# A hybrid decoder layer on one core: block inverse per pair of heads, earlier chains, another order of head groups

## The chip, the core and the metric

The kernel runs on one core of a Trainium2 chip. The core has TensorE (PE, with its weight loads as PEld), VectorE (DVE), ScalarE (ACT), GpSimd (POOL) and SyncE (SP); each runs its own instructions in order and waits for the others by semaphores. The metric is the device time of one execution in microseconds (us), as a median of several runs. A profile of one execution stands beside it.

## What is computed

A decoder layer on 16 meta tokens and 256 tokens of width 2048, in float32. Eight pairs of heads go through RWKV-7 time mixing, eight through stick-breaking attention; then come an output projection, LayerNorm, a gated MLP with a convolution, and LayerNorm. The part that matters here is the recurrence of the time mixing:

```python
def step(S, inp):
    r_t, dec_t, k_t, v_t, kk_t, a_t = inp
    sa = jnp.einsum('bhvk,bhk->bhv', S, -kk_t)
    S = (S * dec_t[:, :, None, :] + sa[..., None] * (kk_t * a_t)[:, :, None, :]
         + v_t[..., None] * k_t[:, :, None, :])
    return S, jnp.einsum('bhvk,bhk->bhv', S, r_t)
...
p = h @ w_in[l]
y_rwkv = rwkv7_mixer(p[..., :RWKV_COLS], ...)
y_sb = stick_breaking_mixer(p[..., RWKV_COLS:], sb_norm_g[l])
mix = jnp.concatenate([y_rwkv, y_sb], axis=-1) @ w_out[l]
h = layer_norm(DEEPNORM_ALPHA * h + mix, ln1_g[l], ln1_b[l])
```

## The kernel before

The layer runs in one pass. Weights come by SP's DMA queue in pieces of 512 KB; ACT and DVE split each into a high and a low part (`whi`, line 183, and `wlo`, line 186), and PE makes three products per tile of them (lines 479 to 483 inside the woven part, 227 to 229 outside of it). The stages are: embedding LayerNorm and the small projections (to about 62 us), the woven part (to about 564 us), the rest of the output projection with LayerNorm, the up projection, and the down projection (to the end).

**The woven part.** `ORDER` lists 16 groups: R0 to R7, each a pair of heads of the time mixing, and S0 to S7, each a pair of the stick-breaking attention ("sticks"). Each group has three projections, each of 48 matmuls on PE. Between them the small work is woven in: `weave` counts matmuls, and after every 16 of them a slot comes (`SLOT`), in which tasks that are due may put their next part into PE's order. A task says with `yield` after how many slots it wants to go on. So the order of PE is fixed when the program is built (`manual_schedule` holds it), while the other engines' orders are set by a scheduler. PE can't pass over an instruction that waits.

**One pair of the time mixing.** The 288 padded tokens are 9 blocks of 32 (`NCH`, `CH`). `rwkv_front` makes the decays and the normalised keys (its product `ss` is a head-wise sum on PE). `rwkv_back` makes the `gram` products of each block on PE (line 621) and masks them on DVE (AG, line 623). The upper half of a block's gram is a strictly triangular 32 x 32 matrix, and the chain needs the inverse of one minus it. POOL computes that inverse: two DMAs write the masked blocks to DRAM (`dl`, line 628), others load them as `LT` (line 631) with one block on each partition, and `inverse` then runs 31 steps of two instructions (lines 670 and 672): multiply a column of `Y` with a row of `LT` into `ytmp`, add it to `Y`. `Y` begins as the identity, loaded from a constant (line 601). The result goes to DRAM (`dy`, line 673) and from there to `TT` (line 678).

Before, this is done for two pairs of heads at once: two pairs are 36 blocks (`NB`), and each block stands on three partitions (`RG`) of which each holds 11 of the 32 rows (`NR`): row n on group n modulo 3. That is 108 partitions. `blocks` gives the two pairs one `LT` and one `Y`, and `inverse` runs when the second pair's blocks are loaded.

**The chains.** `chain(q)` walks the 9 blocks for pairs 2q and 2q+1: on PE a product with AG (line 697), one with the inverse TT (line 706), one that moves the state on (line 718), with copies on ACT and DVE between. It begins when `rwkv_back` of the odd pair has ended, and its first yield is `INVERSE` = 18 slots, so that the inverse has time. TT has two buffers, one for even and one for odd q. LT, Y and ytmp have one each.

Other names: `wide` hands out large tiles from two pools and chooses the pool by how many are in use; `mix` tiles are what the output projection reads; `MEAN` says after which of the steps of the first up projection (three matmuls each) the sums of x and of x squared (p1 and p2, line 1038) are taken on PE; POOL adds up what they read (lines 973 and 974).

Of the kernel before, what the change touches and what calls it, by code (L numbers as in the profile page):

```python
# [9 lines left out]
F32 = mybir.dt.float32  # L10
F32R = mybir.dt.float32r
AF = mybir.ActivationFunctionType
ALU = mybir.AluOpType
PSUM = bass.MemoryType.PSUM

P = 128
# [9 lines left out]
CH = 32  # L26
NCH = TP // CH
# [5 lines left out]
NEG = -1.0e30  # L33
EARLY = 8
SLOT = 16
INVERSE = 18
UNITS = 16
MEAN = 8
LATER = 8
AHEAD = 300  # L40
WARM = 42
# [4 lines left out]
GN_EPS, SB_EPS = 64e-5, 1e-6  # L46
ALPHA = 2.0 ** 0.25
DECAY = float(np.exp(-0.5))
NB = 36
RG = 3  # L50
NR = 11

ORDER = [(x[0], int(x[1])) for x in "R0 R1 R2 R3 S0 S1 R4 R5 S2 R6 R7 S3 S4 S5 S6 S7".split()]

KTS = [0, 1, 2, 3, 4, 5, 8, 9, 10, 11, 12, 13, 6, 7, 14, 15]
SBW = NQ + 144 + 16
# [8 lines left out]
for _name, _w in _PV:  # L65
# [4 lines left out]
_CV = [("ident", 128), ("maskg", 2 * CH), ("sbmask", SBW), ("reset", TP),  # L70
       ("tri", 128), ("bd", 128), ("cen", 128), ("ones", 128), ("y0", NR * CH)]
CV = {}
# [7 lines left out]
def constants():  # L80
    c = np.zeros((P, NCV), np.float32)

    def put(name, a):
        o, w = CV[name]
        c[: a.shape[0], o:o + w] = a

    i = np.arange(P)
    put("ident", np.eye(P))
    put("bd", (i[:, None] // 64 == i[None] // 64) / 32)
    put("ones", np.ones((P, P)))  # L90
    put("tri", i[:, None] >= i[None])
    s, t, kind = i[:, None] % CH, i[None, :2 * CH] % CH, i[None, :2 * CH] // CH
    put("maskg", np.where(kind == 0, s < t, s <= t))
    put("cen", np.eye(P) - (i[:, None] // 64 == i[None] // 64) / 64)
    m = np.full((P, SBW), NEG, np.float32)
    for n, (k0, c0, c1, q0) in enumerate(ZB):
        key, q = k0 + i[:, None], q0 + np.arange(c1 - c0)[None]
        ok = key < q
        if n == 2:
            ok &= key >= 256  # L100
        m[:, c0:c1][ok] = 0
    put("sbmask", m)
    r = np.ones((P, TP))
    r[:, ::CH] = 0
    put("reset", r)
    y0 = np.zeros((RG, NB, NR, CH))
    for n in range(CH):
        y0[n % RG, :, n // RG, n] = 1
    put("y0", y0.reshape(RG * NB, NR * CH))
    return c  # L110

# [2 lines left out]
def hybrid_layer(ctx, tc, xin, cst, pvec, w2a2, g2, ln2, w_in, w_out, w_up, w_down, out, dbg=None):  # L114
    nc = tc.nc
    V, S, G, PE = nc.vector, nc.scalar, nc.gpsimd, nc.tensor
    mm = PE.matmul

    def pool(stack, name, **kw):
        return stack.enter_context(tc.tile_pool(name=name, bufs=1, reuse_waits="tile", **kw))  # L120
# [117 lines left out]
    def mtile(dtype, name):  # L238
        return hp.tile([P, 2, TP], dtype, tag="m", bufs=2 * NPAIR, name=name)
# [6 lines left out]
    ncc, nce = CV["y0"][0], CV["tri"][0]  # L246
# [37 lines left out]
    with ExitStack() as es:  # L284
# [88 lines left out]
        o = PV["mu_r"][0]  # L373
# [64 lines left out]
    dp = pool(astack, "dp", space=bass.MemoryType.DRAM)  # L438
# [3 lines left out]
    FULL, SQUARE, HALF_COLS, QUARTER_COLS = range(4)  # L442
# [51 lines left out]
    used = [NPAIR, 0]  # L494
# [5 lines left out]
    def persistent(name, shape):  # L500
        t = ap2.tile(shape, F32, name=name)
        G.memset(t, 0.0)
        return t


    TT = [persistent(f"TT{p}", [P, NCH, 2 * CH]) for p in range(2)]
# [3 lines left out]
    def atile(name, shape, bufs=1):  # L510
        return ap2.tile(shape, F32, tag=name, bufs=bufs, name=name)
# [11 lines left out]
    urow = [slice(64, 96), slice(0, 32)]  # L523
# [25 lines left out]
    def wide(name, dtype=F32, n=None):  # L549

        if n is None:
            n = int(used[1] < UNITS)
        place_of[name] = n
        used[n] += 1
        assert used[n] <= (2 * NPAIR, UNITS)[n], (name, place_of)
        return mtile(dtype, name) if n == 0 else ap2.tile([P, 2, TP], dtype, tag="m", bufs=UNITS, name=name)

    def rwkv_front(j, st):

        a = sg[j][:, 1]  # L560
        sq = atile("sq", [P, TP])
        S.activation(sq, k_, AF.Square, scale=par("k_k", j))
        sq = halves(sq, "rn", "ss")
        cum = atile("cum", [P, TP])
        V.tensor_tensor_scan(out=cum, data0=reset, data1=sg[j][:, 0], initial=0.0, op0=ALU.mult, op1=ALU.add)
        S.activation(Pt[:, :, 1:], ch(cum), AF.Exp, scale=-DECAY)
        Pinv = cum
        S.activation(Pinv, cum, AF.Exp, scale=DECAY)
        yield 2, FULL, 1
        ps = misc("ss")  # L570
        by_head(ps[:, :TP], *sq)
        ss = atile("ss", [P, TP])
        V.tensor_scalar(out=ss, in0=ps[:, :TP], scalar1=16.0, scalar2=0.5e-24, op0=ALU.mult, op1=ALU.max)
        rn = atile("rn", [P, TP])
        S.activation(rn, ss, AF.Ln, scale=2.0 * KSC)
        S.activation(rn, rn, AF.Exp, scale=-0.5, bias=lnb[:, 1:2])
        y2 = atile("sq", [P, TP])
        S.activation(y2, rn, AF.Square)
        V.tensor_mul(ss, ss, y2)
        V.scalar_tensor_tensor(rn, ss, 1.5, rn, op0=ALU.subtract, op1=ALU.mult)  # L580
        kkn = rn
        V.scalar_tensor_tensor(kkn, k_, par("k_k", j), rn, op0=ALU.mult, op1=ALU.mult)
        ba = atile("ss", [P, TP])
        V.scalar_tensor_tensor(ba, kkn, -1.0, a, op0=ALU.mult, op1=ALU.mult)
        kp = st["kp"] = atile("kp", [P, TP])
        S.activation(kp, a, AF.Identity, scale=par("k_a", j), bias=omka[:, j:j + 1])
        give(f"sg{j}")
        V.tensor_mul(kp, kp, k_)
        BK = st["BK"] = wide(f"BK{j}", n=0).rearrange("p n t -> p (n t)").rearrange("p (c x t) -> p c x t", x=2, t=CH)
        V.tensor_mul(BK[:, :, 0], ch(ba), ch(Pinv))  # L590
        V.tensor_mul(BK[:, :, 1], ch(kp), ch(Pinv))
        st["kkn"] = kkn

    solved, bonus = {}, {}
    dl = dp.tile([4, NCH, CH, CH], F32, name="dl")
    dy = dp.tile([NB, NR * RG, CH], F32, name="dy")

    def blocks(q):
        if q not in solved:
            solved[q] = atile("LT", [P, CH, CH]), atile("Y", [P, NR, CH])  # L600
            nc.gpsimd.dma_start(solved[q][1][:RG * NB].rearrange("p r t -> p (r t)"), cst[:RG * NB, ncc:])
        return solved[q]

    def rwkv_back(j, st):

        BK = st["BK"].rearrange("p c x t -> p c (x t)")
        AG = st["AG"] = [wide(f"AG{j}{x}").rearrange("p n t -> p (n t)").rearrange("p (c t) -> p c t", c=NCH) for x in range(2)]
# [15 lines left out]
                V.tensor_mul(AG[x][t, c0:c0 + n], ps[t, :n], maskg[t].unsqueeze(1).to_broadcast([64, n, 2 * CH]))  # L623

        V.tensor_mul(BK, BK, PC.unsqueeze(2).to_broadcast([P, NCH, 2 * CH]))
        LT, Y = blocks(j // 2)
        for x in range(2):
            nc.gpsimd.dma_start(dl[j % 2 * 2 + x].rearrange("c s t -> s c t"), AG[x][urow[x], :, :CH])
        for g in range(RG):
            o = g * NB + j % 2 * 2 * NCH  # L630
            nc.gpsimd.dma_start(LT[o:o + 2 * NCH], dl[j % 2 * 2:j % 2 * 2 + 2].rearrange("x c s t -> (x c) s t"))
        if j % 2:
            inverse(j // 2, LT, Y)
        yield 1, FULL, 1
        ps = misc("bonus")
        by_head(ps[:, :NQ], *rk)
# [23 lines left out]
        for h, t in zip(heads, toks):  # L660
            V.tensor_copy(BT[t, NCH - 1], pv_[:64, 3, h])

    def inverse(q, LT, Y):

        tmp = atile("ytmp", [P, NR, CH])
        n_ = RG * NB
        for s in range(CH - 1):
            n = s // RG + 1
            m = CH - 1 - s
            G.tensor_tensor(out=tmp[:n_, :n, :m], in0=Y[:n_, :n, s:s + 1].to_broadcast([n_, n, m]),  # L670
                            in1=LT[:n_, s:s + 1, s + 1:].to_broadcast([n_, n, m]), op=ALU.mult)
            G.tensor_tensor(out=Y[:n_, :n, s + 1:], in0=Y[:n_, :n, s + 1:], in1=tmp[:n_, :n, :m], op=ALU.add)  # L672
        nc.gpsimd.dma_start(dy.rearrange("b (g r) t -> g b (r t)", g=RG), Y[:n_].rearrange("p r t -> p (r t)"))
        for n in range(4):
            x, o = n % 2, n * CH
            for g in range(RG):
                k = len(range(g, CH, RG))
                nc.gpsimd.dma_start(TT[q % 2][o + g:o + CH:RG, :, CH - x * CH:2 * CH - x * CH],
                                    dy[n * NCH:n * NCH + NCH, g * NR:g * NR + k].rearrange("c r t -> r c t"))

    def first_of_all():
        return tc.high_priority(offset=AHEAD)
# [1 line left out]
    def chain(q):  # L684
# [7 lines left out]

        yield INVERSE, QUARTER_COLS, 0
        for c in range(NCH):
# [177 lines left out]
    state = [dict() for _ in range(NPAIR)]  # L872
    for kind, j in ORDER:
        st = state[j]
# [11 lines left out]
        else:  # L886
            qkv = []
            for n in range(3):
# [4 lines left out]
                if n == 2:  # L893
                    t = atile("sbin", [P, T])
                    S.copy(t, ps[:, :T])
                else:
                    t = stacked(ps, n)
# [18 lines left out]
    for i in range(EARLY):  # L916
# [3 lines left out]
        x = hs[i][:, 0, :NQ]  # L920
# [57 lines left out]
    for i in range(EARLY):  # L978
        hi, lo = weight(wi + i // 2)
        ps = bank(f"o{i}b")  # L980
        for n in range(4):
            m = mix[kts[12 + n]]
# [7 lines left out]
    for i in range(EARLY, KT):  # L990
        ps = bank(f"o{i}")
        for hf in range(2):
            hi, lo = weight(wi)
            wi += 1
            for kk in range(8):
                n = hf * 8 + kk
                m = mix[kts[n]]
# [6 lines left out]
        x = hs[i][:, 0, :NQ]  # L1004
# [24 lines left out]
    for n, (m, kt) in enumerate(steps):  # L1029
# [3 lines left out]
        if n == 47:  # L1033
            weight(first["up"] + 7, ahead=0)
        if n == MEAN:
            p1, p2 = bank("p1", "st", 2), bank("p2", "st", 2)
# [174 lines left out]
def layout(inputs):  # L1211
# [67 lines left out]
```

## Time and profile before

| | us |
|---|---|
| median of 3 runs (1411.16 to 1415.84) | 1411.25 |
| the profiled execution, its own time | 1412.04 |
| its span, first to last instruction | 1410.3 |
| PE busy in the span | 1336.0 |
| POOL busy in the span | 251.9 |
| mean clock granted to PE, as a share of full speed | 0.971 |

The busy time of an engine is no measure of how close it is to the end's path. PE's order is fixed, so its waits count one for one, whoever else is idle. POOL works for 18% of the span, but in the woven part PE waits for what it makes.

### The profile page before, as it was taken

What the parts mean: (1) busy time and instruction counts of PE and PEld (TensorE: products, weight loads), DVE (VectorE), ACT (ScalarE), POOL (GpSimd) and SP (SyncE); (2) the same over time, 40 slices, a digit from 0 to 9 for tenths busy, and PEclk for the clock granted to TensorE, in tenths of its full rate; (3) what the DMA queues carried; (4) which work ended last, traced back from release to release, by engine and by line L of the source; (5) the groups of instructions that cost most, each with busy time, mean ns of one, the idle gap of its engine ahead of it and who ended that gap; (6) DMA issues with size and microseconds to landing.
All of it is one profiled execution on the core that took longest, in us unless ns stands there. A gap on an engine that the chain in (4) does not pass through costs nothing.

```text
span 1410.3 us, 25107 instructions
## 1 busy us (share of the span) xinstructions
PE 1336.0 (95%) x9900; PEld 1221.5 (87%) x9900; DVE 943.1 (67%) x1546; ACT 729.5 (52%) x1263; POOL 251.9 (18%) x449
## 2 busy tenths in 40 slices
PE   8999898789999999988999999999999999999996
PEld 5988797789789889987999999999999988888895
DVE  7688577778876877798755556665656654444545
ACT  6756455457556756455644444545445443343331
POOL 4107772046172000453100000000000000000002
PEclk8999899899999999999999999999999999999999
DMA  7444433234343324543465655665655666555662
GB/s 235 133 142 130 142 117 99 84 107 140 118 126 114 113 91 154 159 145 124 152 206 162 198 189 180 193 195 184 188 183 180 185 217 214 198 186 189 198 191 94
DMA packets 68662, 223.96 MB, mean 159 GB/s; under 512 B 9912, under 2 KB 12148, under 8 KB 68400
## 3 DMA queue, kind: packets, MB, share of 16 engines
q1 hardware_dynamic: 63392, 215.03, 47.9%
q0 software_dynamic: 4288, 4.19, 1.5%
q10 hardware_dynamic: 864, 3.15, 0.6%
q8 instruction: 77, 1.26, 0.4%
q14 instruction: 41, 0.34, 0.1%
HBM read 219.01 MB, written 3.30 MB: 158 GB/s over the span
## 4 chain that ended last, share of the span: by engine, by line
PE 68%; DVE 9%; issue 3%; POOL 3%; ACT 2%; DMA 2%; POOLq 0%; DVEq 0%; ACTq 0%
PE u L1138 11%; PE u L229 6%; PE u L227 6%; PE u L228 6%; PE d L1159 6%; PE d L1158 6%; PE d L1160 6%; PE u L1139 5%; DVE wlo L186 3%; PE S L481 2%; PE S L483 2%; PE S L479 2%; ACT whi L183 1%; POOL ytmp L670 1%; POOL Y L672 1%
## 5 line engine op out<-in xcount | busy, mean ns | idle before, releaser
L186 DVE TENSOR_TENSOR wlo<-wraw,whi 128x1024 fp32r<-128x1024 f32 (+1 forms) x396 | 484.1, 1228 | 365.6 <-ACT whi L183 362.5
L183 ACT CAST whi<-wraw 128x1024 fp32r<-128x1024 f32 (+1 forms) x396 | 409.0, 1039 | 470.6 <-DMA wraw<-in_w_up_dram 143.5
L1138 PE MATMUL u<-h,whi 128*128 128x512 f32 x640 | 228.5, 398 | 0.0
L227 PE MATMUL u<-h,whi 128*128 128x258 f32 (+2 forms) x768 | 220.1, 287 | 1.9 <-ACT whi L183 1.9
L229 PE MATMUL u<-h,wlo 128*128 128x258 f32 (+2 forms) x768 | 217.9, 285 | 2.9 <-DVE wlo L186 2.9
L228 PE MATMUL u<-h,whi 128*128 128x258 f32 (+2 forms) x768 | 217.5, 284 | 0.0
L1139 PE MATMUL u<-h,wlo 128*128 128x256 f32 x640 | 180.1, 281 | 0.0
L229 PEld LDWEIGHTS u<-h,wlo 128*128 128x128 f32 x768 | 147.1, 192 | 4.0 <-DVE wlo L186 4.0
L227 PEld LDWEIGHTS u<-h,whi 128*128 128x128 f32 x768 | 146.4, 191 | 4.4 <-ACT whi L183 2.5
L228 PEld LDWEIGHTS u<-h,whi 128*128 128x128 f32 x768 | 147.1, 192 | 0.1
L1159 PE MATMUL d<-wlo,ahi 128*128 128x512 f32 (+1 forms) x396 | 145.7, 368 | 0.0
L1158 PE MATMUL d<-whi,ahi 128*128 128x512 f32 (+1 forms) x396 | 145.6, 368 | 0.0
L1160 PE MATMUL d<-whi,alo 128*128 128x512 f32 (+1 forms) x396 | 145.3, 367 | 0.0
L1138 PEld LDWEIGHTS u<-h,whi 128*128 128x128 f32 x640 | 120.6, 189 | 27.6
L1173 POOL TENSOR_TENSOR drs<-drs,mhalf 128x1 f32<-128x1 f32 x2 | 2.1, 1038 | 713.4 <-DVE drs L1172 713.4
L1139 PEld LDWEIGHTS u<-h,wlo 128*128 128x128 f32 x640 | 121.4, 190 | 0.0
L479 PE MATMUL S<-h,whi 128*128 128x272 f32 (+1 forms) x384 | 114.6, 298 | 1.6 <-DVE ql L807 1.6
L483 PE MATMUL S<-h,wlo 128*128 128x272 f32 (+1 forms) x384 | 114.7, 299 | 0.0
L481 PE MATMUL S<-h,whi 128*128 128x272 f32 (+1 forms) x384 | 114.7, 299 | 0.0
L479 PE MATMUL R<-h,whi 128*128 128x272 f32 (+1 forms) x352 | 106.3, 302 | 2.4 <-DVE shv L269 2.4
L483 PE MATMUL R<-h,wlo 128*128 128x272 f32 (+1 forms) x352 | 105.6, 300 | 0.0
L481 PE MATMUL R<-h,whi 128*128 128x272 f32 (+1 forms) x352 | 105.4, 300 | 0.0
(393 smaller groups left out, 2625.2 us busy)
## 6 DMA issues: line engine op xcount, KB each, us to landing
wraw<-in_w_up_dram SPq DMA_DIRECT2D x176, 512.0 KB, 3.9
wraw<-in_w_in_dram SPq DMA_DIRECT2D x96, 512.0 KB, 3.5
wraw<-in_w_down_dram SPq DMA_DIRECT2D x88, 512.0 KB, 4.1
wraw<-in_w_out_dram SPq DMA_DIRECT2D x28, 512.0 KB, 3.5
xraw<-in_w_in_dram SPq DMA_DIRECT2D x12, 256.0 KB, 3.8
xt<-in_xin_dram SPq DMA_DIRECT2D x8, 256.0 KB, 5.2
wraw<-in_w_out_dram SPq DMA_DIRECT2D x8, 256.0 KB, 2.5
l<-in_ln_dram ACTq DMA_DIRECT2D x1, 2048.0 KB, 8.2
```

The source lines that it names most:

```text
L183: S.copy(hi[:, :wide], raw[:, :wide])
L186: V.tensor_sub(lo[:, :wide], raw[:, :wide], hi[:, :wide].bitcast(F32))
L227: mm(ps, lhsT=hi[:, sl], rhs=xh, start=start, stop=False)
L228: mm(ps, lhsT=hi[:, sl], rhs=xl, start=False, stop=False)
L229: mm(ps, lhsT=lo[:, sl], rhs=xh, start=False, stop=stop)
L479: mm(ps, lhsT=hi[:, sl], rhs=xh, start=start, stop=False)
L481: mm(ps, lhsT=hi[:, sl], rhs=xl, start=False, stop=False)
L483: mm(ps, lhsT=lo[:, sl], rhs=xh, start=False, stop=stop)
L1138: mm(ps, lhsT=hi[:, sl], rhs=h1[:, kt, :, 2:NQ], start=kt == 0, stop=False)
L1139: mm(ps[:, :SEQ], lhsT=lo[:, sl], rhs=h1[:, kt, 0, 2:NQ], start=False, stop=kt == KT - 1)
L1158: mm(ps, lhsT=ahi[:, f, t_], rhs=hi[:, w], start=f == 0, stop=False)
L1159: mm(ps, lhsT=ahi[:, f, t_], rhs=lo[:, w], start=False, stop=False)
```

## The change

The inverse is made per pair of heads: 18 blocks, each on seven partitions with five rows each, 126 partitions in all, and the rows of a group are now neighbours (row n on group n divided by 5). Each pair has its own `LT`, `Y` and run of 62 instructions, and its own half of the DRAM buffer `dy`; LT is loaded by seven DMAs in place of three, and TT by two for each pair in place of twelve for two pairs. `ytmp` is written as one flat run. The first yield of a chain goes from 18 to 13 slots. In `ORDER` a stick follows each two pairs. `ss` stands one slot further back. `wide` takes the first pool while it holds fewer than 11. The sums p1 and p2 stand behind step 20 in place of step 8.

```diff
-INVERSE = 18
+INVERSE = 13
 UNITS = 16
-MEAN = 8
+MEAN = 20
...
-NB = 36
-RG = 3
-NR = 11
-
-ORDER = [(x[0], int(x[1])) for x in "R0 R1 R2 R3 S0 S1 R4 R5 S2 R6 R7 S3 S4 S5 S6 S7".split()]
+NB = 18
+RG = 7
+NR = 5
+
+ORDER = [(x[0], int(x[1])) for x in "R0 R1 S0 R2 R3 S1 R4 R5 S2 R6 R7 S3 S4 S5 S6 S7".split()]
...
-        y0[n % RG, :, n // RG, n] = 1
+        y0[n // NR, :, n % NR, n] = 1
...
-            n = int(used[1] < UNITS)
+            n = int(used[0] >= 11 and used[1] < UNITS)
...
-        yield 2, FULL, 1
+        yield 3, FULL, 1
         ps = misc("ss")
...
-    dy = dp.tile([NB, NR * RG, CH], F32, name="dy")
-
-    def blocks(q):
-        if q not in solved:
-            solved[q] = atile("LT", [P, CH, CH]), atile("Y", [P, NR, CH])
-            nc.gpsimd.dma_start(solved[q][1][:RG * NB].rearrange("p r t -> p (r t)"), cst[:RG * NB, ncc:])
-        return solved[q]
+    dy = dp.tile([2, NB, NR * RG, CH], F32, name="dy")
...
-        LT, Y = blocks(j // 2)
+        LT, Y = atile("LT", [P, CH, CH]), atile("Y", [P, NR, CH])
+        nc.gpsimd.dma_start(Y[:RG * NB].rearrange("p r t -> p (r t)"), cst[:RG * NB, ncc:])
+        here = dl[j % 2 * 2:j % 2 * 2 + 2]
         for x in range(2):
-            nc.gpsimd.dma_start(dl[j % 2 * 2 + x].rearrange("c s t -> s c t"), AG[x][urow[x], :, :CH])
+            nc.gpsimd.dma_start(here[x].rearrange("c s t -> s c t"), AG[x][urow[x], :, :CH])
         for g in range(RG):
-            o = g * NB + j % 2 * 2 * NCH
-            nc.gpsimd.dma_start(LT[o:o + 2 * NCH], dl[j % 2 * 2:j % 2 * 2 + 2].rearrange("x c s t -> (x c) s t"))
-        if j % 2:
-            inverse(j // 2, LT, Y)
+            nc.gpsimd.dma_start(LT[g * NB:g * NB + NB], here.rearrange("x c s t -> (x c) s t"))
+        inverse(j, LT, Y)
...
-    def inverse(q, LT, Y):
-
-        tmp = atile("ytmp", [P, NR, CH])
+    def inverse(j, LT, Y):
+
+        part = [(min(s + 1, NR), CH - 1 - s) for s in range(CH - 1)]
+        flat = atile("ytmp", [P, max(n * m for n, m in part)])
         n_ = RG * NB
-        for s in range(CH - 1):
-            n = s // RG + 1
-            m = CH - 1 - s
-            G.tensor_tensor(out=tmp[:n_, :n, :m], in0=Y[:n_, :n, s:s + 1].to_broadcast([n_, n, m]),
+        for s, (n, m) in enumerate(part):
+            tmp = flat[:n_, :n * m].rearrange("p (n m) -> p n m", m=m)
+            G.tensor_tensor(out=tmp, in0=Y[:n_, :n, s:s + 1].to_broadcast([n_, n, m]),
                             in1=LT[:n_, s:s + 1, s + 1:].to_broadcast([n_, n, m]), op=ALU.mult)
-            G.tensor_tensor(out=Y[:n_, :n, s + 1:], in0=Y[:n_, :n, s + 1:], in1=tmp[:n_, :n, :m], op=ALU.add)
-        nc.gpsimd.dma_start(dy.rearrange("b (g r) t -> g b (r t)", g=RG), Y[:n_].rearrange("p r t -> p (r t)"))
-        for n in range(4):
-            x, o = n % 2, n * CH
-            for g in range(RG):
-                k = len(range(g, CH, RG))
-                nc.gpsimd.dma_start(TT[q % 2][o + g:o + CH:RG, :, CH - x * CH:2 * CH - x * CH],
-                                    dy[n * NCH:n * NCH + NCH, g * NR:g * NR + k].rearrange("c r t -> r c t"))
+            G.tensor_tensor(out=Y[:n_, :n, s + 1:], in0=Y[:n_, :n, s + 1:], in1=tmp, op=ALU.add)
+        there = dy[j % 2]
+        nc.gpsimd.dma_start(there.rearrange("b (g r) t -> g b (r t)", g=RG), Y[:n_].rearrange("p r t -> p (r t)"))
+        for x in range(2):
+            o = j % 2 * 64 + x * CH
+            nc.gpsimd.dma_start(TT[j // 2 % 2][o:o + CH, :, CH - x * CH:2 * CH - x * CH],
+                                there[x * NCH:x * NCH + NCH, :CH].rearrange("c r t -> r c t"))
```

POOL's order where the blocks of the first two pairs come in, before (AG10 and AG11 are the masked grams of pair 1):

```order
L628 DMA dl_871<-AG00_967 32x9x32 [waits DVE_49]
L628 DMA dl_871<-AG01_968 32x9x32 [waits DVE_49]
L631 DMA LT_1066<-dl_871 18x1024 [waits DMASW2_49,DMASW1_49]
L631 DMA LT_1066<-dl_871 18x1024 x2
L628 DMA dl_871<-AG10_1265 32x9x32 [waits DVE_49]
L628 DMA dl_871<-AG11_1266 32x9x32 [waits DVE_49]
L631 DMA LT_1066<-dl_871 18x1024 [waits DMASW7_49,DMASW6_49,DMASW0_49]
L631 DMA LT_1066<-dl_871 18x1024 x2
L670 TENSOR_TENSOR ytmp_1369<-Y_1067,LT_1066 108x31 [waits DMASW3_49,DMASW4_49,DMASW2_49,DMASW5_49,DMASW1_49,DMASW0_49]
L672 TENSOR_TENSOR Y_1067<-Y_1067,ytmp_1369 108x31 [waits Pool_49]
```

And now, at the end of pair 0's inverse (LT_1434 and Y_1435 are pair 1's tiles):

```order
L664 TENSOR_TENSOR ytmp_1078<-Y_1067,LT_1066 126x5 [waits Pool_49]
L666 TENSOR_TENSOR Y_1067<-Y_1067,ytmp_1078 126x5 [waits Pool_49]
L626 DMA LT_1434<-dl_871 18x1024 [waits DMASW3_49,DMASW2_49]
L668 DMA dy_872<-Y_1067 7x18x160 [waits Pool_49]
L626 DMA LT_1434<-dl_871 18x1024 x2
L671 DMA TT0_864<-dy_872 32x9x32 [waits DMASW5_49]
L671 DMA TT0_864<-dy_872 32x9x32
L621 DMA Y_1435<-in_cst_dram 126x160
L626 DMA LT_1434<-dl_871 18x1024
L626 DMA LT_1434<-dl_871 18x1024 [waits DMASW4_49]
L626 DMA LT_1434<-dl_871 18x1024
L626 DMA LT_1434<-dl_871 18x1024 [waits DMASW6_49]
```

The loads of pair 1's blocks now stand behind the last operation of pair 0's inverse, four of them also behind the wait for pair 0's dy; before, they stood ahead of the one inverse.

PE's order at the first product with TT, before:

```order
L706 MATMUL chain_2253<-Wt_2222,TT0_864 64x64 x2
L481 MATMUL S02_2230<-h5_78,whi40_1979 128x272
L483 MATMUL S02_2230<-h5_78,wlo40_1981 128x272
L479 MATMUL S02_2230<-h6_79,whi40_1979 128x272
L481 MATMUL S02_2230<-h6_79,whi40_1979 128x272
```

And now:

```order
L699 MATMUL chain_2021<-Wt_1981,TT0_864 64x64 x2
L481 MATMUL R31_1998<-h5_78,whi36_1833 128x272
L483 MATMUL R31_1998<-h5_78,wlo36_1835 128x272
L479 MATMUL R31_1998<-h6_79,whi36_1833 128x272
L481 MATMUL R31_1998<-h6_79,whi36_1833 128x272
```

It stood in the last projection of the first stick, behind the grams of pairs 0 to 3 (1078 matmuls ahead of it); now it stands in the first projection of pair 3, behind the grams of pairs 0 and 1 alone (957 matmuls), and the gram of pair 2 follows it. Counted in matmuls from the program's start, the first product of chains 0 to 3 with TT has 957, 1606, 2271 and 2937 ahead of it now, and 1078, 1462, 2391 and 3031 before; the grams of pairs 0, 2, 4 and 6 now have 460, 997, 1648 and 2313.

## Rows read from the trace of the kernel before

**Rows 1.** The page, busy time of each engine (share of span) xinstructions

```profile
PE 1336.0 (95%) x9900; PEld 1221.5 (87%) x9900; DVE 943.1 (67%) x1546; ACT 729.5 (52%) x1263; POOL 251.9 (18%) x449
```

**Rows 2.** Windows at chain 0's wait: us, PE PEld DVE ACT POOL busy, clock, DMA

```profile
161.00:168.60 7.60, 1.00 (x7) 0.62 (x6) 1.86 (x3) 0.51 (x2) 7.18 (x13) 0.72 0.41 99
168.60:174.60 6.00, 6.00 (x31) 5.51 (x32) 1.67 (x3) 2.27 (x7) 2.77 (x5) 0.50 0.31 76
```

**Rows 3.** Waits of PE: us in total, times, longest

```profile
PE chain L706 <- DMA TT<-dy: 11.4, 4, 5.5
...
PE p L1038 <- POOL s L974: 2.7, 1, 2.7
...
PE o0b L227 <- ACT mix L749: 2.4, 1, 2.4
```

**Rows 4.** Timeline of PE: start us, us, instruction, count, idle before and releaser

```profile
76.14 0.33 PE L621 MATMUL gram<-AG,BK 64*64 64x64 f32 x2
...
166.88 0.44 PE L706 MATMUL chain<-Wt,TT 64*64 64x64 f32 x2 [5.46 <-DMA TT<-dy]
...
226.52 0.44 PE L706 MATMUL chain<-Wt,TT 64*64 64x64 f32 x2 [3.78 <-DMA TT<-dy]
...
362.72 0.33 PE L706 MATMUL chain<-Wt,TT 64*64 64x64 f32 x4
...
446.06 0.33 PE L706 MATMUL chain<-Wt,TT 64*64 64x64 f32 x4
```

**Rows 5.** Timeline of POOL, first inverse and the DMAs around it

```profile
81.46 1.33 POOL L628 DMA_DIRECT2D dl<-AG  x2 [17.80 <-DVE AG L623]
85.16 1.54 POOL L631 DMA_DIRECT2D LT<-dl  x3 [2.37 <-DMA dl<-AG]
...
115.55 0.78 POOL L670 TENSOR_TENSOR ytmp<-Y,LT 108x31 f32<-108x31 f32 x1 [4.00 <-DMA LT<-dl]
...
153.61 0.23 POOL L672 TENSOR_TENSOR Y<-Y,ytmp 108x11 f32<-108x11 f32 x1
154.14 0.79 POOL L673 DMA_DIRECT2D dy<-Y  x1 [0.30 <-POOL Y L672]
...
159.97 6.98 POOL L678 DMA_DIRECT2D TT<-dy  x12 [4.40 <-DMA dy<-Y]
166.95 0.60 POOL L601 DMA_DIRECT2D Y<-in_cst_dram  x1
...
217.30 6.99 POOL L678 DMA_DIRECT2D TT<-dy  x12 [5.34 <-DMA dy<-Y]
```

**Rows 6.** POOL's operations by line; min/median/max ns; two of 30 elements

```profile
L672 POOL TENSOR_TENSOR Y<-Y,ytmp 108x84 f32<-108x84 f32 (+23 forms) x124 | 57.3, 462 | 9.7
L670 POOL TENSOR_TENSOR ytmp<-Y,LT 108x84 f32<-108x84 f32 (+23 forms) x124 | 55.9, 451 | 22.4 <-DMA LT<-dl 7.0 <-issue 6.0
...
L670 POOL TENSOR_TENSOR ytmp<-Y,LT x124: 214/336/2294, 115.6 to 423.2; 108x84 f32<-108x84 f32 x12, 108x30 f32<-108x30 f32 x8, 108x54 f32<-108x54 f32 x8, 108x72 f32<-108x72 f32 x8
L672 POOL TENSOR_TENSOR Y<-Y,ytmp x124: 231/344/1361, 116.4 to 423.5; 108x84 f32<-108x84 f32 x12, 108x30 f32<-108x30 f32 x8, 108x54 f32<-108x54 f32 x8, 108x72 f32<-108x72 f32 x8
...
116.74 0.24 POOL L670 TENSOR_TENSOR ytmp<-Y,LT 108x30 f32<-108x30 f32 x1
...
151.13 0.24 POOL L670 TENSOR_TENSOR ytmp<-Y,LT 108x30 f32<-108x30 f32 x1
...
L973 POOL TENSOR_TENSOR s<-s,x x15: 727/925/1723, 590.7 to 637.5; 128x258 f32<-128x258 f32 x15
```

**Rows 7.** DMAs of dy and of LT: issue ns, then issue to landing us

```profile
L673 POOL DMA_DIRECT2D dy<-Y x4: 787/787/793, 154.1 to 424.0; - x4
...
DMA to landing us min/median/max: 5.6/5.8/6.4
...
L631 POOL DMA_DIRECT2D LT<-dl x24: 498/522/541, 85.2 to 389.7; - x24
...
DMA to landing us min/median/max: 2.3/3.3/5.0
```

More of the change, by code (lines that the diff above doesn't have):

```diff
@@ L592, in rwkv_front @@
         st["kkn"] = kkn
-    solved, bonus = {}, {}
+    bonus = {}
     dl = dp.tile([4, NCH, CH, CH], F32, name="dl")
-    dy = dp.tile([NB, NR * RG, CH], F32, name="dy")
-    def blocks(q):
-        if q not in solved:
-            solved[q] = atile("LT", [P, CH, CH]), atile("Y", [P, NR, CH])
-            nc.gpsimd.dma_start(solved[q][1][:RG * NB].rearrange("p r t -> p (r t)"), cst[:RG * NB, ncc:])
-        return solved[q]
+    dy = dp.tile([2, NB, NR * RG, CH], F32, name="dy")
     def rwkv_back(j, st):
```

## The prediction

> **What bounds the kernel now.** The page's first section comes first: TensorE (PE) is busy 95% of the span and, apart from its own weight loads, no other engine over 67% [rows 1]. PE runs in an order that is written out by hand, so every wait of PE is time on the end. The table of waits of PE says where the rest goes: the longest group is the chains' product with the block inverse, 11.4 us in four waits for the DMA that brings TT back [rows 3]. The others are smaller; of those that the change touches, one of 2.7 us is for the second of two sums (POOL) and one of 2.4 us for the last mix tile. PE's clock matters too: after the first TT wait it was granted 0.50, the lower of its two levels (1.2 of 2.4 GHz), for 6.0 us, which costs 3.0 us [rows 2]. The instructions of PE and their sizes are the same before and after; the order alone differs. So the question is when TT lands and when PE asks for it.
>
> **When PE asks.** Positions are counted along PE's program order, in matmuls ahead. Before, pair 0's gram has 460 ahead and starts at 76.14 us, and chain 0 asks for TT with 1078 ahead, at 161.42 (166.88 less its 5.46 of waiting) [rows 4]: 618 matmuls in 85.3 us, 0.138 us each. In the changed order chain 0 asks with 957 ahead, 497 behind that gram, which stands where it stood: 497 x 0.138 = 68.6, so it is due at 144.7, 17 us earlier. For chains 1 to 3 the pace is that from chain 2 to chain 3 before: 640 matmuls from 362.72 to 446.06 [rows 4], 0.130 each. In the changed order a chain asks 609, 623 and 624 matmuls behind the gram of its first pair: **due 80 us behind it**. That gram stands 40 to 42 matmuls (5.5 us) behind the TT product of the chain before, and PE is in order: it can't run until that TT is there.
>
> **What POOL needs, gram to TT.** Before, one inverse of 62 instructions serves two pairs: four in all. Now each pair has one: eight. LT, Y and ytmp have one buffer each, so the second pair's LT loads stand behind the last operation of the first inverse (the order of POOL in the section on the change). Step by step:
> - Gram to the first dl issue 5.3 us (76.14 to 81.46), to the LT issues 3.7, seven LT issues instead of three, 1.54/3 each, 3.6, and 4.0 until the first operation [rows 4, 5]: **16.6**.
> - One inverse. The 248 operations before were busy 57.3 + 55.9 us; a fourth of that is 28.3, and 62 gaps of 0.078 (9.7/124) make **33.1**; the first one took 38.3 (115.55 to 153.84) [rows 5, 6]. Size: the free elements go from 1991 to 2180 in each of the two lines. From 0.24 us at 30 elements to 0.727 at 258 is 2.1 ns per element [rows 6], so +0.8. Partitions cost nothing (the 258 row has 128), and 108x30 takes 0.24 both as one run of 30 and as ten runs of 3, so writing ytmp flat gains nothing either. I take 33.9, and for the first of all 36.5, between 33.9 and 39.1, since DVE is as busy there.
> - The second pair's two dl issues, 1.3, fall into the first inverse.
> - Hand-over to the second inverse: 0.3, dy's landing, two TT issues 1.2 (6.98/12 each), Y 0.6, four LT issues 2.1, landing 4.0. dy's landing took 5.8 for 152 KB; now it is 81 KB, and LT with 74 KB lands in 3.3 [rows 5, 7]. I take 4.6, the middle. Sum **12.8**.
> - Second inverse. While PE stood at TT, DVE was busy 1.86 of 7.6 us [rows 2], and POOL's long operations (up to 2.3 us against a median of 0.34) come beside a busy DVE [rows 6]. With all at the median an inverse takes 31 x 0.680 + 4.8 + 0.8 = 26.7. The Trainium skill (SBUF — State Buffer, "Who interferes with whom") states the reason: a DVE instruction with two SBUF inputs and a GpSimd instruction that reads SBUF lock each other out for a whole instruction. By that rule an inverse that runs while PE waits should approach 26.7; without it, 33.9 would stand and the sum would be some 19 us higher. For chain 0 the second inverse starts at 143.3, just as PE stops: 27. For the others it starts 64.6 behind the gram, 15 us before PE stops: 30.
> - Last TT: 0.3 + 4.6 + 1.2 + 2.2 until it is seen (224.29 to 226.52) [rows 4, 5]: **8.3**.
>
> Chain 0: 16.6 + 36.5 + 1.3 + 12.8 + 27 + 8.3 = 102.5 behind 76.1, so TT lands at 178.6, **34 us late**. Chains 1 to 3: 16.6 + 33.9 + 1.3 + 12.8 + 30 + 8.3 = 102.9 against 80, **23 us late each**. TT's twelve small DMAs became four, which saves 4.7 us, but one more inverse, one more dy round trip and eight more LT loads stand on the same path.
>
> The Trainium skill (DMA: Bandwidth & Descriptors, "Anatomy of one DMA") gives about 2.0 us plus bytes over 436 GB/s for a POOL DMA, by which dy would land in 2.2 us and eight landings would take 19 us off the sum (about 1470). The row of dy, 5.8 us where the formula gives 2.4, speaks against it.
>
> **The sum.** Chain 3 gets TT at 178.6 + 3 x (5.5 + 3.0 for the half clock behind a wait + 102.9) = 512.8, against 446.1 before: +66.7. From there PE has 94 matmuls more to go than before (3031 less 2937), x 0.130 = +12.2, and once more 3.0 for the clock. Gains behind it: the two sums are asked for 12 steps (36 matmuls of 0.12 us, 4.3 us) later, which hides the 2.7; the price is that what hangs on them starts no later than now, since the sums end when they did. Chain 3 and its gate products end earlier before the out projection, which hides the 2.4. So -5.1. All waits of PE ahead of chain 3 (the old TT waits, the ss products that now stand a slot later, the sticks set between pairs) no longer count: POOL sets the time there, and that includes the pool choice in `wide` and the new head order, which I cost at nothing for this reason; if POOL did not, they would be worth a few us of gain. Total +76.8 on the profiled execution's 1412.0 (span 1410.3 and 1.7 around it; 0.8 over the median 1411.25): **1489 us**.
>
> **Rivals.**
> - POOL runs free: PE's waits leave DVE idle, all inverses take 26.7 and dy lands in 3.3. Path 89.8, chain 3 at 76.1 + 89.8 + 3 x 98.3 = 461, end at 1437. For it: the medians. Against: the first inverse and the first 15 us of the second lie beside a PE, and so a DVE, that works. The opposite end, 39.1 for each inverse and 5.8 for dy, gives path 119.6 and 1556.
> - Other side, **faster**: per-pair inverses are short enough to be ready. Apart from the inverses the path is 39, so the point is two inverses in 41 us, 20.5 each: 0.253 us an operation. Then chains 1 to 3 don't wait. The old 11.4 of TT waits, about 6 of half clock behind them and 5.1 go; chain 0 is still 11 late: 1412 - 22.5 + 11 = 1400. For it: the smallest operations take 0.21 to 0.24. Against: the median is 0.34 [rows 6], and the new instructions have more elements, up to 135.
> - No change: the lateness is eaten by the other waits of PE, and the time stays at 1412. It would need paths of 92 us at chain 0 and 85 at the others; chance small.
>
> **Chances and range.** Forecast (1440 to 1520) 0.62; POOL free (about 1437) 0.20; slower still 0.06; ready in time 0.08; no change 0.04. Range 1430 to 1520, which leaves out the faster and unchanged cases, the slow end and part of the second. About 0.5% is what a measurement of this kernel can tell: faster 0.08, same 0.04, slower 0.88.
>
> **What would show it.** The changed profile should have four long PE waits at the TT product of the chains for DMA TT, the first the longest (about 34 us, then 23 each); eight groups of 62 POOL operations of 27 to 37 us; the second of each pair starting some 13 us behind the first's end; half clock behind each wait; no wait at the two sums. An operation mean near 0.25 us, or a second inverse that is done when PE asks, would make the prediction wrong.

## Result and profile after

The changed kernel takes 1492.83 us (median of 4 runs, 1488.42 to 1496.87) against 1411.2: a ratio of 1.0569 with a 95% interval of 1.0528 to 1.0611. Its profiled execution took 1495.5 us, 83.5 more than that of before. The page shows PE as busy as before in time and less in share [rows 1], and POOL busy 111 us longer. In the chain that ended last POOL now has 16% of the span.

```profile
PE 1336.3 (89%) x9900; PEld 1221.1 (82%) x9900; DVE 947.7 (63%) x1546; ACT 732.8 (49%) x1263; POOL 363.1 (24%) x705
...
PE 61%; POOL 16%; DVE 9%; DMA 6%; issue 5%; ACT 3%; POOLq 0%; SPq 0%; DVEq 0%; ACTq 0%
```

The table of PE's waits (total us, times, longest) answers to [rows 3]. The chains' product waits 77.9 us for TT in place of 11.4. The waits at p1 and p2 and at the last mix tile are gone. Below the TT line stand waits that were smaller before or not there.

```profile
PE chain L699 <- DMA TT<-dy: 77.9, 4, 35.0
PE gram L615 <- DVE gsq L544: 7.8, 2, 4.1
PE vt L645 <- ACT BT L650: 6.6, 3, 2.4
PE o L229 <- DVE wlo L186: 5.1, 3, 2.2
PE gate L776 <- ACT BT L650: 4.3, 2, 2.5
PE z L819 <- DVE prn L858: 4.0, 2, 3.3
```

PE's timeline at the first product of each chain with TT answers to [rows 4]:

```profile
179.00 0.45 PE L699 MATMUL chain<-Wt,TT 64*64 64x64 f32 x2 [35.00 <-DMA TT<-dy]
...
287.97 0.45 PE L699 MATMUL chain<-Wt,TT 64*64 64x64 f32 x2 [19.26 <-DMA TT<-dy]
...
399.95 0.44 PE L699 MATMUL chain<-Wt,TT 64*64 64x64 f32 x2 [12.60 <-DMA TT<-dy]
...
509.17 0.44 PE L699 MATMUL chain<-Wt,TT 64*64 64x64 f32 x2 [11.04 <-DMA TT<-dy]
```

POOL's timeline in chain 0 answers to [rows 5]. It shows the first operation of pair 0's inverse, the hand-over to pair 1's, the end of that one, and then what follows: 13.09 us without work until the gram of pair 2, which stands behind PE's wait, has come through DVE.

```profile
93.73 0.23 POOL L664 TENSOR_TENSOR ytmp<-Y,LT 126x31 f32<-126x31 f32 x1 [4.12 <-DMA LT<-dl]
...
134.97 0.57 POOL L626 DMA_DIRECT2D LT<-dl  x1
135.53 0.67 POOL L668 DMA_DIRECT2D dy<-Y  x1
...
139.37 1.27 POOL L671 DMA_DIRECT2D TT<-dy  x2 [2.13 <-DMA dy<-Y]
...
141.19 2.00 POOL L626 DMA_DIRECT2D LT<-dl  x4
...
172.83 0.71 POOL L668 DMA_DIRECT2D dy<-Y  x1 [0.30 <-POOL Y L666]
176.03 1.25 POOL L671 DMA_DIRECT2D TT<-dy  x2 [2.49 <-DMA dy<-Y]
...
190.91 1.21 POOL L624 DMA_DIRECT2D dl<-AG  x2 [13.09 <-DVE AG L617]
```

The windows over the first four inverses (columns as in [rows 2]) show the same 62 operations at four lengths; POOL's counts of 65 and 64 in the first and the third take in DMA issues that fall between them. In the second PE, ACT and DVE do nothing.

```profile
93.70:135.00 41.30, 38.03 (x330) 37.39 (x330) 32.79 (x52) 26.65 (x50) 36.61 (x65) 1.00 0.49 154
...
148.10:172.50 24.40, 0.00 (x0) 0.00 (x0) 0.00 (x0) 0.00 (x0) 19.59 (x62) 0.50 0.00 0
...
203.00:239.00 36.00, 33.29 (x310) 29.82 (x308) 29.84 (x63) 18.05 (x37) 31.30 (x64) 0.95 0.35 106
252.00:282.00 30.00, 16.71 (x204) 15.59 (x204) 16.38 (x32) 9.31 (x19) 25.16 (x62) 0.86 0.22 71
```

### The profile page after: what moved, and what is told of

The parts are those of the page before. It is cut to its first block, busy times and chain, and to the rows that moved or that the text cites. A ratio compares the mean times of both kernels' runs of the same rounds, so it can differ in the third digit from the quotient of the medians.

```text
span 1493.7 us, 25367 instructions
## 1 busy us (share of the span) xinstructions
PE 1336.3 (89%) x9900; PEld 1221.1 (82%) x9900; DVE 947.7 (63%) x1546; ACT 732.8 (49%) x1263; POOL 363.1 (24%) x705
## 4 chain that ended last, share of the span: by engine, by line
PE 61%; POOL 16%; DVE 9%; DMA 6%; issue 5%; ACT 3%; POOLq 0%; SPq 0%; DVEq 0%; ACTq 0%
PE u L1131 10%; POOL ytmp L664 7%; POOL Y L666 7%; PE u L229 6%; PE u L227 6%; PE u L228 6%; PE d L1152 5%; PE d L1151 5%; PE d L1153 5%; PE u L1132 5%; DVE wlo L186 2%; DMA LT<-dl 2%; DMA dy<-Y 1%; POOL LT L626 1%; PE S L481 1%
## 5 line engine op out<-in xcount | busy, mean ns | idle before, releaser
L664 POOL TENSOR_TENSOR ytmp<-Y,LT 126x60 f32<-126x60 f32 (+29 forms) x248 | 110.8, 447 | 54.9 <-DMA LT<-dl 36.2
L479 PE MATMUL S<-h,whi 128*128 128x272 f32 (+1 forms) x384 | 117.2, 305 | 0.0
L481 PE MATMUL S<-h,whi 128*128 128x272 f32 (+1 forms) x384 | 116.9, 304 | 0.0
L666 POOL TENSOR_TENSOR Y<-Y,ytmp 126x60 f32<-126x60 f32 (+29 forms) x248 | 111.2, 449 | 19.3
L479 PE MATMUL R<-h,whi 128*128 128x272 f32 (+1 forms) x352 | 105.4, 300 | 2.9 <-DVE shv L269 2.9
```

The costliest lines, as they stand in the source:

```text
L479: mm(ps, lhsT=hi[:, sl], rhs=xh, start=start, stop=False)
```

## Experiments

The theory: POOL's path of two inverses for each chain sets when TT lands, and because the next pair's gram stands behind PE's wait for TT, POOL and PE wait for each other in turn. The rival: the earlier ask and the new order cost the time, whoever makes the inverse. The waits for TT by chain (the first two TT products of a chain summed) and the medians, each ratio to runs of before on the same chip (the kernels are described one by one below):

| kernel | TT waits at chains 0 to 3, us | median us | ratio (95%) |
|---|---|---|---|
| before | 6.6, 4.9, 0, 0 | 1411.2 | 1 |
| changed | 35.0, 19.3, 12.6, 11.0 | 1492.8 | 1.0569 (1.0528 to 1.0611) |
| oldinv13 | 21.2, 12.5, 2.1, 6.3 | 1449.5 | 1.0255 (1.0217 to 1.0293) |
| oldinv15 | 17.3, 2.2, 1.1, 0 | 1414.5 | 1.0012 (0.9988 to 1.0036) |
| pairinv3 | 18.0, 27.8, 0, 1.5 | 1458.2 | 1.0294 (1.0260 to 1.0327) |
| after14 | 33.2, 17.9, 10.2, 11.8 | 1482.0 | 1.0482 (1.0460 to 1.0503) |
| after15 | 31.3, 9.9, 1.9, 0 | 1451.9 | 1.0277 (1.0238 to 1.0317) |
| halfinv | 10.0, 0, 0, 0 | 1423.0 | 1.0080 (1.0059 to 1.0101) |
| twobufm | 30.9, 17.6, 9.0, 8.6 | 1495.4 | 1.0560 (1.0527 to 1.0593) |

**The change without its inverse (oldinv13).** Against the kernel before:

```diff
-INVERSE = 18
+INVERSE = 13
-MEAN = 8
+MEAN = 20
-ORDER = [... "R0 R1 R2 R3 S0 S1 R4 ...
+ORDER = [... "R0 R1 S0 R2 R3 S1 R4 ...
-            n = int(used[1] < UNITS)
+            n = int(used[0] >= 11 and used[1] < UNITS)
-        yield 2, FULL, 1
+        yield 3, FULL, 1
```

> All of the change but its main part: chains at 13 slots, the new order of the head groups, ss a slot further back, the new pool choice and the sums behind step 20, but with the old inverse (two pairs at once, four inverses in all). Theory, POOL's doubled inverse path is the cause: TT lands about 62 us behind the gram of the second pair (in the trace of before), the ask comes 405 to 410 matmuls, 53 us, behind that gram at chains 1 to 3 and 323 matmuls, 45 us, at chain 0. So waits of about 22 us at chain 0 and 9 us at chains 1 to 3, and about 1430 us (1415 to 1445), most of the loss gone. Rival, the loss comes from asking 5 slots earlier and from the new order of the groups, whoever makes the inverse: TT waits near those of the changed kernel (35, 19, 13, 11) and 1470 to 1495.

Neither was right: 1449.5, above the first range and below the second. The TT waits sum to 42.1 us, near the 49 expected, but 13 slots brought waits elsewhere too, those of the changed kernel:

```profile
PE chain L706 <- DMA TT<-dy: 42.1, 7, 18.4
...
PE gram L621 <- DVE gsq L544: 4.4, 2, 2.2
...
PE z L826 <- DVE prn L865: 4.0, 2, 3.3
```

So all of the change but its inverse costs about 2.5%.

**The inverse alone (pairinv_only, pairinv3).** The kernel before with the new `inverse`, NB, RG, NR and `dy`, and nothing else of the change; then the same with a third TT:

```diff
-    TT = [persistent(f"TT{p}", [P, NCH, 2 * CH]) for p in range(2)]
+    TT = [persistent(f"TT{p}", [P, NCH, 2 * CH]) for p in range(3)]
-            nc.gpsimd.dma_start(TT[j // 2 % 2]...
+            nc.gpsimd.dma_start(TT[j // 2 % 3]...
-        T_ = TT[q % 2]
+        T_ = TT[q % 3]
```

> The kernel before with the inverse per pair alone: old order of the head groups, chains at 18 slots, ss, pools and sums as before. Theory, the doubled inverse path on POOL sets the time: the grams of pairs 0 to 3 all stand ahead of the first product with TT, so POOL runs four inverses in a row, and each costs some 30 to 36 us and a hand-over of 13. Chain 0 is due 85 us behind its gram and needs 102.5: 17 late; chain 1 about 24 late; chains 2 and 3 have 100 and 94 us between their first gram and the ask and are late by 0 to 9. Sum with 3 us of half clock behind each wait, less the old 11.4 of waits: about +45, 1455 us (1440 to 1475). Rival, the inverse is not the cause but the early ask and the order are: within 1% of before, about 1411.

1496.5, ratio 1.0586 (1.0547 to 1.0626): 40 us over the theory. The third of its four TT waits stands inside chain 0:

```profile
PE chain L699 <- DMA TT<-dy: 88.7, 4, 40.5
...
329.66 0.37 PE L699 MATMUL chain<-Wt,TT 64*64 64x64 f32 x2 [40.52 <-DMA TT<-dy]
```

> As the run with the inverse per pair alone in the kernel before, but with a third TT buffer. In that run the last block of chain 0 stood in PE's order behind the write of pair 4's inverse into the same TT buffer: PE waited 40.5 us there for it (and that block of pair 0 was computed with pair 4's inverse). With three buffers nothing is overwritten early. Theory: the wait of 40.5 us and the half clock behind it go, the waits of 18.7 and 27.4 us at chains 0 and 1 stay, chains 2 and 3 wait 0 to 10 us since POOL isn't given those 40 us to catch up; 1455 us (1445 to 1468). Rival, POOL is behind for good in this order, and chains 2 and 3 take over the 40 us: 1485 or more.

1458.2: the theory's 1455. The 40 us came from two TT buffers in a program order where an inverse is issued with each pair, not from POOL's length. The waits at chains 0 and 1, where four inverses run in a row, came as priced (17 and 24 expected, 18.0 and 27.8 measured). With a third buffer the inverse thus costs 2.9% in the old order, without it 5.9%. That 1.0255 x 1.0294 = 1.056 meets the 1.0569 of the change is a match of totals: chain by chain the waits of the two runs don't add up to those of the changed kernel (at chain 1 they are 12.5 and 27.8, in the changed kernel 19.3).

**The chains two slots and one slot later (after15, after14).** The changed kernel with one number:

```diff
-INVERSE = 13
+INVERSE = 15
```

> The changed kernel with chains at 15 slots in place of 13: the first product of a chain with TT is asked for 50 matmuls (6 to 7 us) later, and by that the gram of the next group's first pair comes to stand 18 matmuls ahead of it in PE's order, where it stood 40 behind. Theory, POOL and PE wait for each other in turn: in the changed kernel a chain's wait holds up the next gram, and POOL lies idle from its last TT issue until that gram has gone through DVE and DRAM (30 us from the end of one chain's second inverse to the start of the next chain's first, where the hand-over inside a chain takes 13). With the gram ahead of the wait POOL goes on at once, so the distance from chain to chain falls from 110 us to about 34 + 31 + 2 x 14 = 93 us: 3 x 17 less, about 1448 us (1435 to 1465). Rival A, POOL's own work alone sets the time, wherever the grams stand: 1493, since the same 8 inverses are to be made. Rival B, only the time of the ask counts: each wait 6 to 7 us shorter but the chains 7 us later too, 1485 to 1495.

> The changed kernel with chains at 14 slots: the control for the run with 15. The first product with TT is asked for 18 matmuls later, but the next pair's gram still stands behind it (18 matmuls behind, where 13 slots have 40 and 15 slots have it 18 ahead). Theory, the wait matters because the next gram stands behind it: only the 22 matmuls (3 us) less between TT and gram are won at each of three chains, 9 us in all: 1484 us (1478 to 1490), with chain 0's wait some 33 us. Rival, each slot later is worth the same, whatever stands behind: half of the 41 us that 15 slots brought, 1472.

1451.9 and 1482.0: both as the theory said, and the rivals of both runs fell. One slot is worth 10.9 us, the next 30.1 (12 and 29 by the ratios to before). In the run with 15 the gram stands ahead of PE's wait, and POOL's wait for its masked form falls from 13.09 to 4.04 us:

```profile
148.95 1.09 PE L615 MATMUL gram<-AG,BK 64*64 64x64 f32 x30
...
181.54 0.44 PE L699 MATMUL chain<-Wt,TT 64*64 64x64 f32 x2 [31.33 <-DMA TT<-dy]
...
178.58 1.25 POOL L671 DMA_DIRECT2D TT<-dy  x2 [2.50 <-DMA dy<-Y]
...
184.43 1.21 POOL L624 DMA_DIRECT2D dl<-AG  x2 [4.04 <-DVE AG L617]
...
195.45 0.23 POOL L664 TENSOR_TENSOR ytmp<-Y,LT 126x31 f32<-126x31 f32 x1 [4.10 <-DMA LT<-dl]
```

From the second inverse's end to the next first one POOL needs 20.3 us (175.1 to 195.4) in place of 30.5 (172.5 to 203.0). The table of POOL's waits has it in one row, 60.0 us in the changed kernel, 30.3 with 15 slots:

```profile
POOL dl L624 <- DVE AG L617: 60.0, 6, 19.4
...
POOL dl L624 <- DVE AG L617: 30.3, 4, 19.4
```

The distance from chain to chain fell from 109 and 112 us to 100.5 and 98, not to 93: 20.3 us is still more than a hand-over of 13.

**Half of each inverse (halfinv).**

```diff
-        for s, (n, m) in enumerate(part):
+        for s, (n, m) in list(enumerate(part))[::2]:
```

> The changed kernel with every second elimination step of each inverse left out (16 steps of two operations in place of 31), so part of the computation is left out and an inverse takes about half as long, 15 to 18 us; DMAs, grams, order and slots as in the changed kernel. Theory, the length of the inverses makes the waits: gram to TT becomes 16.6 + 18 + 1.3 + 12.8 + 15 + 8.3 = 72 us, against an ask 68.6 us behind the gram at chain 0 (3 us late) and 80 at the others (in time). All long waits go, 1395 to 1412 us. Rival, the DMAs (seven LT loads for each pair, dy and TT there and back) or the early ask are the cause: waits of over 10 us stay at most chains and the time stays above 1450.

The waits went as expected (one is left, 10.0 us at chain 0; the inverses took 15 to 22 us), so it is the inverses' length that makes them; the DMAs are those of the changed kernel. But the time is 1423.0, 11 us above the range, though PE waits 1.4 us less for TT than before. All rows of the table of PE's waits sum to 69.9 us, where before they sum to 60.7. What is left are the small ones of the changed kernel:

```profile
PE chain L699 <- DMA TT<-dy: 10.0, 1, 10.0
PE gram L615 <- DVE gsq L544: 6.3, 2, 3.3
...
PE gate L776 <- ACT BT L650: 4.3, 2, 2.5
...
PE z L819 <- DVE prn L858: 4.0, 2, 3.3
```

**The old inverse at 15 slots (oldinv15).** As oldinv13, with `INVERSE = 15`.

> All of the change but the inverse, as the first run with the old inverse, with chains at 15 slots in place of 13: the question is what the new order of the groups, ss, the pools and the sums are worth when the inverse is nearly in time. Theory: chain 0 asks at about 150 and TT lands at 161, 11 us late; chains 1 to 3 ask 60 us behind the gram of their second pair, as long as TT takes, so they wait 0 to 3 us; the changed order's own waits (gram on gsq, vt, gate and z, seen in the run with half inverses) stay: 1420 to 1430 us, slower than before. Rival, the order is worth a gain once POOL doesn't hold it up: 1400 to 1408.

1414.5, no different from before: better than the theory's range and slower than the rival's. The TT waits came as forecast at chains 1 to 3 (2.2, 1.1 and 0) and longer at chain 0 (17.3, 11 forecast), but those on gsq and on prn and the gate's on BT are not among the long ones here. So the small waits belong to 13 slots, not to the order of the groups: 13 slots cost twice, at TT and elsewhere.

**Two buffers for LT and Y (twobufm).**

```diff
-        LT, Y = atile("LT", [P, CH, CH]), atile("Y", [P, NR, CH])
+        LT, Y = atile("LT", [P, CH - 1, CH], bufs=2), atile("Y", [P, NR, CH], bufs=2)
...
-            nc.gpsimd.dma_start(LT[g * NB:g * NB + NB], here.rearrange("x c s t -> (x c) s t"))
+            nc.gpsimd.dma_start(LT[g * NB:g * NB + NB], here.rearrange("x c s t -> (x c) s t")[:, :CH - 1])
...
-        sq = atile("psq", [P, NQ])
+        sq = atile("gsq", [P, NQ])
...
-        rn = atile("prn", [P, NQ])
+        rn = atile("yh", [P, NQ])
```

> The changed kernel with two buffers for LT and Y (LT without its last row, which nothing reads; for the space, two tags of the sticks share a buffer with tiles of the chains' end). The second pair's LT loads no longer wait for the end of the first inverse. Theory, POOL's instructions and the landings between them fill the path: the landings of dy and LT (3.4 + 4.0 us) leave the hand-over between the two inverses of a chain, the issues (0.5 us each) stay on POOL, and the second inverse runs a little longer beside a busier DVE. The hand-over goes from 13 to 15 us down to 2 to 8, each TT lands 4 to 7 us earlier, in all 16 to 28 us less: about 1472 us (1462 to 1480). Rival, the single buffer is the main cost of the change: 13 us less at each chain, about 1440. Rival, the buffer is of no account: 1493.

No change in time. In chain 0 the hand-over is gone; the second inverse begins 0.7 us after dy's issue:

```profile
139.39 0.69 POOL L668 DMA_DIRECT2D dy<-Y  x1 [0.30 <-POOL Y L666]
140.09 0.66 POOL L664 TENSOR_TENSOR ytmp<-Y,LT 126x31 f32<-126x31 f32 x1
```

Yet TT lands only 3.9 us earlier there (175.1): LT's issues now lie inside the first inverse, and the second begins beside a working DVE and takes 29.1 us in place of 24.4. At chain 3 the gain is 7.1 us, and 8.5 us are lost behind it. PE waits 5.1 us longer there at the gate for `yh`, the tag that the edit shares (3.2 in the changed kernel):

```profile
PE gate L778 <- DVE yh L769: 8.3, 2, 4.3
```

PE is also busy 4.9 us longer behind chain 3, at a lower clock (0.92 in the first 130.8 us, 0.95 in the changed kernel). What two buffers alone would bring can't be told from this run.

**Parts that could help the kernel before.** The sums (`MEAN = 20`) alone; with 20 slots; with `yield 3` ahead of ss; that one with 19 slots.

> The kernel before with one number of the change: the sums p1 and p2 behind step 20 of the first up projection in place of step 8. Theory: PE's wait of 2.7 us for the second sum (and what it costs in clock behind it, up to 1.7) goes and nothing else moves: 1408 to 1410 us, ratio 0.997 to 0.998. Rival, what hangs on the sums becomes late instead: no change, 1412.

> The kernel before with the sums behind step 20 and the chains at 20 slots in place of 18, the opposite direction to the change's 13. Theory: PE asks 52 matmuls, 7 us, later for TT, so all four TT waits (11.4 us with the longest 5.5) and the half clock behind them (3 to 6 us) go; chain 3 ends 7 us later, which may add up to 7 us at the last mix tile before the output projection (2.4 us before). Net with the sums: 1396 to 1404 us. Rival, the wait moves to the end of the woven part in full: 1408 to 1412.

> The kernel before with two numbers of the change, the sums behind step 20 and ss one slot further back. In the run with the sums alone PE waits 8.6 us for the norms of ss (5.5 and 3.1). Theory: a slot more, 16 matmuls or 2 us, hides most of single waits of up to 2.3 us: 5 to 7 us less, 1402 to 1405. Rival, the waits move on, as they did when the chains were set two slots later: the same time as with the sums alone, 1409.

> The faster version of the kernel before (sums behind step 20, ss one slot further back) with chains at 19 slots in place of 18. In that version PE waits 12.7 us at chain 0 for TT and about 1 us at chain 1. Theory: one slot, 16 to 18 matmuls or 2.4 us at chain 0, takes that much of the wait, and the end of the woven part hides one slot: 1394 to 1397 us against 1397.5. Rival, as with two slots more and the old ss, the waits move to the sticks and the gates behind chains 2 and 3: 1398 to 1405.

| kernel | median us | ratio (95%) |
|---|---|---|
| mean20 | 1409.2 | 0.9952 (0.9928 to 0.9975) |
| m20_20 | 1415.1 | 0.9999 (0.9974 to 1.0025) |
| m20y3 | 1397.5 | 0.9891 (0.9876 to 0.9906) |
| m20y3_19 | 1402.7 | 0.9938 (0.9917 to 0.9960) |

The sums brought 3.5 to 10.2 us by the interval, where 2.7 to 4.4 was expected. Both later asks failed: 19 slots came out as the rival said, and with 20 slots the wait for TT falls from 10.1 to 4.0 us, and PE waits at ss, at the bonus and for a stick's tile in its place. In the whole table its waits for TT are 6.1 us shorter than with the sums alone and all others 11.1 longer. The rows of m20_20:

```profile
PE ss L536 <- ACT rn L530: 7.7, 7, 2.1
PE bonus L536 <- DVE AG L623: 6.0, 6, 2.4
PE S L479 <- DVE ql L807: 5.8, 3, 3.0
PE chain L706 <- DMA TT<-dy: 4.0, 3, 2.4
```

The best version is the kernel before with the sums behind step 20 and ss one slot further back: 1.1% faster than before, more than expected. In its table the ss rows of 5.5 and 3.1 us are gone, but the TT wait is 13.2 us and vt's is 7.2:

```profile
PE chain L706 <- DMA TT<-dy: 13.2, 3, 9.8
...
PE vt L651 <- DVE bv L640: 7.2, 3, 2.8
```

The two profiled executions, 1401.7 us with the sums alone and 1399.2, lie much nearer than the medians, since the one lies at the lower end of its runs (1401.7 to 1415.0) and the other at the upper end of its own (1397.1 to 1399.2). The medians are also of two chips (before 1415.9 and 1412.6 there); by the ratios ss is worth some 9 us, not 12. The granted clock differs with the times: 0.978 to 0.981 in the four executions with the later ss, 0.971 to 0.976 in nine of the eleven with the sums alone. Why it is higher stays open.

## Why the prediction was right, and where it was not

- **When TT lands** was right for all chains: 178.6, 290.0, 401.4 and 512.8 forecast, 179.0, 288.0, 400.0 and 509.2 measured. For chain 0 that is in part luck, since terms erred against each other. The first inverse with the two dl issues inside it took 41.3 us (36.5 + 1.3 forecast), the second 24.4 (27), and from its end to TT it took 6.5 (8.3).
- **The second inverse beside an idle DVE.** Its 62 operations were busy 19.6 us; those of the third inverse, beside a DVE busy 29.84 of 36 us, 30.1. The runs with 15 slots and with three TT buffers have inverses of 25.5 and 25.7 us in like stretches. The Trainium skill (SBUF — State Buffer, "Who interferes with whom") names DVE as the cause, and the trace agrees. ACT and PE were idle in those stretches too, so the lengths alone don't single DVE out, but the timelines do. In the first inverse an operation beside ACT's cast and PE's matmuls took 0.29 us; the one that began just behind the start of a DVE instruction with two inputs (wraw and whi) took 1.32:

```profile
122.26 1.05 ACT L183 CAST whi<-wraw 128x1024 fp32r<-128x1024 f32 x1 [0.40 <-PE R L481]
...
122.64 0.29 POOL L664 TENSOR_TENSOR ytmp<-Y,LT 126x55 f32<-126x55 f32 x1
...
123.34 1.23 DVE L186 TENSOR_TENSOR wlo<-wraw,whi 128x1024 fp32r<-128x1024 f32 x1 [2.10 <-ACT whi L183]
123.38 1.32 POOL L664 TENSOR_TENSOR ytmp<-Y,LT 126x50 f32<-126x50 f32 x1
```

  Over all 496 operations of the changed kernel's inverses, 51 took over 0.5 us more than the shortest of their line and shape, and each of the 51 overlaps a DVE instruction on two or more tensors (its name holds TENSOR_TENSOR). The 191 that overlap none took at most 0.02 us more, whatever PE and ACT did.
- **The hand-over**: 13.1, 13.0, 14.6 and 15.7 us against 12.8. dy landed sooner than taken, but the last LT load later, up to 5.6 us (the second row is the landing of dy, the fourth of LT; they answer to [rows 7]). In chains 2 and 3 the second pair's two dl issues, which the prediction put into the first inverse, stand in the hand-over (1.25 us from 346.59 and 1.24 from 457.68), and all seven LT issues follow them:

```profile
L668 POOL DMA_DIRECT2D dy<-Y x8: 673/706/711, 135.5 to 503.3; - x8
...
DMA to landing us min/median/max: 2.5/3.1/4.0
...
L626 POOL DMA_DIRECT2D LT<-dl x56: 498/501/568, 86.1 to 466.3; - x56
...
DMA to landing us min/median/max: 2.3/3.7/5.6
```

  The estimate of 2.2 us for dy from the Trainium skill (DMA: Bandwidth & Descriptors, "Anatomy of one DMA") is below the fastest of the eight landings, 2.5.
- **Waits of 23 us at chains 1 to 3** were too long by 4 to 12 (19.3, 12.6, 11.0). From one TT to the next ask PE took 89.7, 99.4 and 98.2 us where the prediction has 88.5. At chains 2 and 3 it had waited 7.9 and 9.0 us at gsq, vt and the gate by then; at chain 1 TT itself came 2.4 us sooner behind the one before (109.0 us, 111.4 forecast). The later asks cost nothing more, as forecast: POOL set the time, and the landings held.
- **The gains** at p1, p2 and the last mix tile (5.1 us) came.
- **The term that was mis-sized is the stretch behind chain 3's TT.** The prediction put no new wait there; its cost of nothing for the new order held ahead of chain 3 only. From chain 3's TT to the end the forecast was 974.3 us (1410.3 - 446.1 + 12.2 + 3.0 - 5.1), measured 984.5. PE's new waits there are at z (6.9 us, 1.2 before), the gate (3.2, none before) and the first `o` products (5.1, 3.4 before), 10.6 us more in all. The longest of them is z on prn (4.0 us). The runs with 15 slots have 0.4 of it, the old inverse at 13 slots 4.0, so these waits come mostly with the 13 slots. With TT 3.6 us early this leaves the profiled execution 6.5 us over the forecast of 1489.
- **The rival "ready in time"** was priced at 1400 with chain 0 late by 11. The run with half inverses is that case, with 10.0, and took 1423: the same small waits. So even with inverses half as long the change would have been slower than before. The rival that POOL runs free (1437) held for one inverse of the eight.

## To carry to other kernels

Where an engine with a fixed order waits for a helper engine, look at what stands behind that wait: if the helper's next input does, the two run in turn, and moving the wait by one slot, from 18 matmuls ahead of that input to 18 behind it, was worth 30 us here, where the slot before it gave 11. Splitting a job into two to use more partitions (108 to 126) doubled the count of operations while their durations stayed about the same (344 ns median), so it nearly doubled the helper's busy time in them, from 113 to 222 us. Asking later for a wait that is nearly hidden brought no gain here: with 20 slots 6.1 us less at TT came with 11.1 more elsewhere; with 19 slots 5.0 less came with 2.9 more in the profiled execution, the fastest of its eight, and the median still rose by 5, which those waits don't explain.

## What the runs showed of the hardware

One and the same inverse on POOL took from 24.4 to 41.3 us in one execution: no operation over 0.5 us while PE, ACT and DVE stood still, and single operations of up to 2.20 us beside them at work. What lengthened them was DVE at work on two or more tensors: all 51 operations that took over 0.5 us more than the shortest of their shape lie beside such an instruction, and work of PE or ACT alone cost at most 0.02 us. Here a late helper thus got faster, since PE's wait for it left DVE idle. In the same wait PE's granted clock fell to 0.50, the lower level; over the whole span it averaged 0.951, against 0.971 before.
